# Building the right factors of a fast matrix product on ScalarE and by accumulating DMAs instead of GpSimd, in a two-layer hybrid encoder on one core

## The chip, the core and the metric

The program runs on one core of a Trainium2 chip. A core has five engines that each work through a queue of their own, in order: PE (TensorE, matrix products into PSUM), DVE (VectorE), ACT (ScalarE), POOL (GpSimd) and SP (SyncE, which here only issues DMAs). They meet at semaphores. POOL can issue DMAs as well, and those can add what they carry to what lies at their destination. The metric is the device time of one execution in microseconds (us).

## The reference, cut to what matters

Two layers, 656 tokens (528 of a prompt with 16 meta tokens, 128 of eight running streams), 1024 channels, all in float32. Each layer normalises, projects, runs three kinds of heads and adds an output projection; the change is in what follows, the gated feed-forward part:

```python
h2 = rmsnorm(x, p['g_ffn'])
gate, val = jnp.split(h2 @ p['w_up'].astype(x.dtype), 2, axis=-1)      # 2 x 2816 columns
gate_c, ffn_new = causal_dwconv(gate, ffn_past, p['ffn_conv_w'], p['ffn_conv_b'])   # width 3
x = x + (jax.nn.gelu(gate_c) * val) @ p['w_down'].astype(x.dtype)

def rmsnorm(x, g):
    y = xf * lax.rsqrt(jnp.mean(xf * xf, axis=-1, keepdims=True) + EPS)
    return (y * g.astype(jnp.float32)).astype(x.dtype)
```

## The kernel before

The activations lie with channels on the 128 partitions: eight tiles x0 to x7 of 128 channels by 656 tokens. A float32 product is made of three faster ones: ACT rounds a number to a short format (the high part), DVE subtracts that from the number (the low part), and PE multiplies high by high, high by low and low by high (`mm3`, L374). So every weight tile passes ACT and DVE before PE can use it (`w_split`, L360 and L361; four blocks of 128 columns are one unit). The passing units are held in four buffers (`wsp`, the tiles whi and wlo); a unit that is to stay longer can be put in tiles of the general pool (`own=True`, the tiles ghi and glo). The raw weights come through four buffers (`wraw`), which SP fills.

The feed-forward part of a layer has an entry and a long steady stretch. The steady stretch computes the up-projection in pairs of column blocks (a gate pair, then a value pair) by a seven-product scheme of Winograd's kind: 2 by 2 blocks on either side are first added and subtracted, and seven products take the place of eight. The left factors come from weights (`combos`, L961 on POOL, split at L967 on ACT and L968 on DVE). The right factors come from the activations, once in a layer (`factors`): for each k of 0 to 3 the blocks are b11 and b12 (the first and second half of the tokens of x_k) and b21 and b22 (the same of x_(k+4)). The differences are t1 = b12 - b11, t2 = b22 - t1, t3 = b22 - b12 and t4 = b21 - t2; the seven right factors are b11, b21, t2, t3, t4, t1 and b22, and each is split into high and low parts (ACT at L1065, DVE at L1066, tile fh).

The entry, in the order of the program:

1. The last quarter of the output projection (d_ob), tile by tile. DVE adds it to x (L417), ACT squares x (L408, tile sq), POOL adds up the squares (L413; the last of the adds is DVE's), ACT and DVE split x for the first plain products.
2. PE sums the squares over partitions (np_h), ACT and DVE make the factor r from it (L313 to L317). Meanwhile PE runs the plain products of gates 0 and 1 and value 0 (e_u), whose weights lie in ghi and glo.
3. DVE multiplies x0 to x7 by gain and r (L1044). POOL makes t1 and t2, later t3 and t4 (L1052 to L1061). Two of the seven groups of right factors are split (`FE = 2`); the rest after the plain gates.
4. DVE evicts gates 0 and 1 (L1224), ACT and DVE run the convolution (L1088, L1091) and ACT the gelu (L1094). POOL multiplies by r (L1233), DVE multiplies with the value (L1238 to L1240). Value 1 (d_v), then gates 2 and 3 (d_g) run as plain products on PE. The weights of value 1 take passing buffers, those of gates 2 and 3 ghi and glo.
5. The remaining right factors are split, and PE begins on the seven-product scheme: d_v again, for values 2 and 3, whose products are called v010 to v016 below, then d_g for gates 4 and 5, and between them the down-projection (d_dn).

The order in which the instructions of an engine stand is set by a scheduler from the program's order and its own idea of when inputs are ready; from the seven-product scheme on, the orders of DVE and PE are written out by hand (`manual_schedule`). The DMAs that POOL issues in the before kernel are of the same kind as the new ones: L701 adds one SBUF tile to another, L1306 adds a tile to one in HBM.

Of the kernel before, what the change touches and what calls it, by code (L numbers as in the profile page):

```python
# [12 lines left out]
AF = mybir.ActivationFunctionType  # L13
ALU = mybir.AluOpType
# [7 lines left out]
T = 656  # L22
# [3 lines left out]
NFF = 22  # L26
# [11 lines left out]
NPG = 2  # L38
# [119 lines left out]
def trunk_kernel(ctx: ExitStack, tc: tile.TileContext, i: dict, o: dict, depth: int = 2):  # L158
# [12 lines left out]
    V, A, G, PE = nc.vector, nc.scalar, nc.gpsimd, nc.tensor  # L171

    def S(name, dt=F32):
        return slots.tile([128, T], dt, tag="S", name=name)
# [22 lines left out]
    xs = [S(f"x{m}") for m in range(8)]  # L197
# [25 lines left out]
    def par(name, k):  # L223
        c = COLS[name][0] + k
        return cst[:, c:c + 1]
# [96 lines left out]
    def seq(ins):  # L322

        if start["on"]:
            tc.keep_in_program_order(ins)
            start[ins.ins.engine] = ins.ins

    def split(src, g, nm, a=0):
        hi = S(f"hi_{nm}", F32R)
        lo = S(f"lo_{nm}", F32R)  # L330
        if g is None:
            A.copy(hi[:, a:T], src[:, a:T])  # L332
            V.tensor_tensor(out=lo[:, a:T], in0=src[:, a:T], in1=hi[:, a:T].bitcast(F32), op=ALU.subtract)  # L333
        else:
            seq(A.activation(out=hi[:, a:T], in_=src[:, a:T], func=AF.Identity, scale=g))
            seq(V.scalar_tensor_tensor(out=lo[:, a:T], in0=src[:, a:T], scalar=g, in1=hi[:, a:T].bitcast(F32), op0=ALU.mult,
                                       op1=ALU.subtract))
        return hi, lo

    def w_load(w, k0, kt, parts=None):  # L340
        raw = wraw.tile([128, 8, 128], F32, tag="raw", name="raw")
        for a, b in parts or ((0, kt),):
            nc.sync.dma_start(out=raw[:, a:b], in_=w[:, (k0 + a) * 128:(k0 + b) * 128].rearrange("p (k n) -> p k n", n=128))
        return raw
# [4 lines left out]
    def w_split(raw, kt, a=0, own=False):  # L349

        half = 4 if kt in (4, 8) else 3
        units = []
        while a < kt:
            n = min(half, kt - a)
            if own:
                hi, lo = unit_s("ghi"), unit_s("glo")
            else:
                hi = wsp.tile([128, 4, 128], F32R, tag="whi", name="whi")
                lo = wsp.tile([128, 4, 128], F32R, tag="wlo", name="wlo")
            seq(A.copy(hi[:, :n], raw[:, a:a + n]))  # L360
            seq(V.tensor_tensor(out=lo[:, :n], in0=raw[:, a:a + n], in1=hi[:, :n].bitcast(F32), op=ALU.subtract))  # L361
            units += [(hi, lo, m) for m in range(n)]
            a += n
        return units

    def weights(w, k0, kt, own=False):
        return w_split(w_load(w, k0, kt), kt, 0, own)
# [8 lines left out]
    def gemm1(units, ks, rhs, nm, ab, P=PD):  # L376
        ps = P(f"d_{nm}")
        for k in range(len(ks)):
            mm3(ps, units[k], rhs[ks[k]], ab, k == 0, k == len(ks) - 1)
        return ps  # L380

    def gemm(units, ks, rhs, nm, cc=CA, P=PD):

        return [gemm1(units, ks, rhs, f"{c}_{nm}", cc[c], P) for c in range(2)]

    def gemm_group(unit_lists, ks, rhs, nm, cc=CA):

        ps = [[PD(f"e0_{nm}"), PD(f"e1_{nm}")], [PD(f"e2_{nm}"), PB(f"e3_{nm}")], [PB(f"e4_{nm}"), PB(f"e5_{nm}")]]
        last = len(ks) - 1
        for k in range(len(ks)):  # L390
            for m, units in enumerate(unit_lists):
                for c in range(2):
                    mm3(ps[m][c], units[k], rhs[ks[k]], cc[c], k == 0, k == last)
        return ps
# [7 lines left out]
    sq_acc = {}  # L402

    def sq_add(m, ab=(0, T), E=None):

        a, b = ab
        sq = S(f"sq{m}")
        seq(A.activation(out=sq[:, a:b], in_=xs[m][:, a:b], func=AF.Square))  # L408
        if m == 0:
            sq_acc["t"] = sq  # L410
        else:
            t = sq_acc["t"]
            seq((E or (V if m == 7 else G)).tensor_tensor(out=t[:, a:b], in0=t[:, a:b], in1=sq[:, a:b], op=ALU.add))  # L413

    def add_x(m, ps, cc=CA):
        for c, (a, b) in enumerate(cc):
            V.tensor_tensor(out=xs[m][:, a:b], in0=ps[c][:, :b - a], in1=xs[m][:, a:b], op=ALU.add)  # L417

    def x_out(m):
        nc.sync.dma_start(out=xdr[m], in_=xs[m][:, :T])  # L420
# [616 lines left out]
    def factors(l, r, cc):  # L1037

        (a0, a1), (b0, b1) = cc
        w = a1 - a0  # L1040
        src = []
        for k in range(4):
            for m in (k, k + 4):
                V.scalar_tensor_tensor(out=xs[m][:, a0:T], in0=xs[m][:, a0:T], scalar=par("g_ffn", 8 * l + m),  # L1044
                                       in1=r[:, a0:T], op0=ALU.mult, op1=ALU.mult)
            b11, b12 = xs[k][:, a0:a1], xs[k][:, b0:b1]
            b21, b22 = xs[k + 4][:, a0:a1], xs[k + 4][:, b0:b1]
            t = S(f"ft{l}{k}")
            t1, t3 = t[:, :w], t[:, HC:HC + w]
            t = S(f"fu{l}{k}")  # L1050
            t2, t4 = t[:, :w], t[:, HC:HC + w]
            G.tensor_tensor(out=t1, in0=b12, in1=b11, op=ALU.subtract)  # L1052
            G.tensor_tensor(out=t2, in0=b22, in1=t1, op=ALU.subtract)
            src.append((b11, b21, t2, t3, t4, t1, b22))
        out = [[] for k in range(4)]
        for n in range(7):
            for k in range(4):
                b11, b21, t2, t3, t4, t1, b22 = src[k]
                if n == 1:
                    G.tensor_tensor(out=t3, in0=b22, in1=xs[k][:, b0:b1], op=ALU.subtract)  # L1060
                    G.tensor_tensor(out=t4, in0=b21, in1=t2, op=ALU.subtract)  # L1061
                x = src[k][n]
                t = S(f"fh{l}{k}{n}", F32R)
                hi, lo = t[:, :w], t[:, HC:HC + w]
                A.copy(hi, x)  # L1065
                V.tensor_tensor(out=lo, in0=x, in1=hi.bitcast(F32), op=ALU.subtract)  # L1066
                out[k].append((hi, lo))
            yield out

    def by_stream(x):  # L1070
        return x.rearrange("p (s n) -> p s n", s=8)
# [40 lines left out]
    ks8 = list(range(8))  # L1112
    for l in range(depth):
# [7 lines left out]
        if l == 0:  # L1121
            hs = []
# [20 lines left out]
        ps3 = gemm_group(w3, ks8, hs, f"i{l}")  # L1143
# [21 lines left out]
        for n in range(3, 24):  # L1165
            advance(front)
            ps = gemm(nxt, ks8, hs, f"i{l}{n}")
# [11 lines left out]
        cx, cy = (CB, CC) if l == depth - 1 else (CA, CA)  # L1179
# [7 lines left out]
        for m in range(8):  # L1187
            advance(front)
            x_in(m, xsrc)
            ps = gemm(nxt, ka, mix, f"oa{l}{m}", cx)  # L1190
# [8 lines left out]
        hs = []  # L1199
        wu = i["w_up"][l]  # L1200
        w3 = [weights(wu[n], 0, 8, True) for n in (0, 1, NFF)]
        for m in range(8):
            ps = gemm(nxt, kb, mix, f"ob{l}{m}", cx)
            add_x(m, ps, cx)
            x_out(m)
            sq_add(m, (cx[0][0], T))
            hs.append(split(xs[m], par("g_ffn", 8 * l + m), f"h2{l}{m}", cx[0][0]))
            if m < 7:
                nxt = weights(wo[m + 1], 6, 2)
        r = norm_r(onesd[:, 0], [sq_acc["t"]], f"h2{l}", cx)  # L1210
        ps3 = gemm_group(w3, ks8, hs, f"u{l}", cx)
        gout = S(f"gout{l}")[:, :NFF * 18].rearrange("p (f n) -> p f n", f=NFF)
        wd = i["w_down"][l]
        a0, cw = cy[0][0], cx[0][1] - cx[0][0]
        gates, vals, gts = {}, {}, {}
        fac = factors(l, r, cx)
        for n in range(FE):
            tm = next(fac)
# [7 lines left out]

        for ft in range(2):
            plain_gate(ft, ps3[ft])
        wg = [weights(wu[ft], 0, 8, True) for ft in range(2, 2 + NPG)]
        for ft in range(2):  # L1230
            ps = ps3[2] if ft == 0 else gemm(weights(wu[NFF + 1], 0, 8), ks8, hs, f"v{l}1", cx, PB)
            a, av = gates.pop(ft)
            G.tensor_tensor(out=a[:, a0:TP], in0=a[:, a0:TP], in1=r[:, a0:TP], op=ALU.mult)  # L1233
            G.tensor_tensor(out=av, in0=av, in1=by_stream(r[:, TP:T]), op=ALU.mult)
            v = vals[ft] = S(f"gv{l}{ft}")
            (c0, c1), (d0, _) = cx
            n0 = TP - d0
            V.tensor_tensor(out=v[:, a0:c1], in0=ps[0][:, a0 - c0:c1 - c0], in1=a[:, a0:c1], op=ALU.mult)  # L1238
            V.tensor_tensor(out=v[:, d0:TP], in0=ps[1][:, :n0], in1=a[:, d0:TP], op=ALU.mult)
            V.tensor_tensor(out=by_stream(v[:, TP:T]), in0=by_stream(ps[1][:, n0:n0 + 128]), in1=av, op=ALU.mult)  # L1240
# [87 lines left out]
        for p in range(1, NFF // 2):  # L1328
            for up in (up_gate, up_val)[1 if p == 1 else 0:]:
                for st in up(p):  # L1330
# [3 lines left out]
                    while due and due[0][0] <= nprod:  # L1334
                        _, n, j = due.pop(0)
# [28 lines left out]
        if l < depth - 1:  # L1364
            hs = []
# [10 lines left out]
    for c, (a, b) in enumerate(CF):  # L1376
# [3 lines left out]
        for m in range(8):  # L1380
# [4 lines left out]
            ps = gemm1(wl[m], ks, gts, f"fin{c}{m}", (a, b))  # L1385
# [28 lines left out]
```

## Time and profile before

| | us |
|---|---|
| median of three runs (1696.43 to 1701.21) | 1698.6 |
| the profiled execution | 1697.38 |
| its span, first to last instruction | 1695.6 |
| entry of layer 0, from the last add of step 1 to the first product of step 5 | 393.5 to 439.6 |
| entry of layer 1, the same | 1217.4 to 1262.1 |

The profile is one execution. A row of a timeline gives the start in us from the start of the span, the duration, engine, line, operation, the tiles written and read, the shape, and in brackets how long the engine stood idle before it and what it waited for. Rows of one kind that follow each other are merged, with their count. A duration of a row includes the tail of the last instruction; of instructions that follow each other the next starts some 0.08 us before it ends. PEclk is the granted clock of PE as a share of full speed.

### The profile page before, as it was taken

What the parts mean: (1) busy time and instruction counts of PE and PEld (TensorE: products, weight loads), DVE (VectorE), ACT (ScalarE), POOL (GpSimd) and SP (SyncE); (2) the same over time, 40 slices, a digit from 0 to 9 for tenths busy, and PEclk for the clock granted to TensorE, in tenths of its full rate; (3) what the DMA queues carried; (4) which work ended last, traced back from release to release, by engine and by line L of the source; (5) the groups of instructions that cost most, each with busy time, mean ns of one, the idle gap of its engine ahead of it and who ended that gap; (6) DMA issues with size and microseconds to landing.
All of it is one profiled execution on the core that took longest, in us unless ns stands there. A gap on an engine that the chain in (4) does not pass through costs nothing.

```text
span 1695.6 us, 28745 instructions
## 1 busy us (share of the span) xinstructions
PE 1625.4 (96%) x10772; PEld 1532.0 (90%) x10772; DVE 1238.9 (73%) x2380; ACT 878.7 (52%) x1744; POOL 581.7 (34%) x668
## 2 busy tenths in 40 slices
PE   7999999998999999999999999999999999999985
PEld 6898888898899999999998978789888999999984
DVE  6579985769877767766648898776898767776444
ACT  5656576553545444444445647575454444444343
POOL 0102220008466554553001122100476555554423
PEclk9999999999999999999999999999999999999998
DMA  5236431342145344444612555214411344344442
GB/s 205 90 96 159 115 99 36 112 154 79 50 112 119 100 105 106 102 102 107 221 65 89 128 130 122 67 65 136 144 38 60 95 120 107 101 102 98 119 110 94
DMA packets 75003, 180.56 MB, mean 106 GB/s; under 512 B 12752, under 2 KB 18384, under 8 KB 74864
## 3 DMA queue, kind: packets, MB, share of 16 engines
q1 hardware_dynamic: 62192, 149.36, 27.3%
q0 software_dynamic: 12672, 29.37, 11.1%
q8 instruction: 84, 1.38, 0.3%
q14 instruction: 55, 0.45, 0.1%
HBM read 129.80 MB, written 35.46 MB: 97 GB/s over the span
## 4 chain that ended last, share of the span: by engine, by line
PE 78%; DVE 10%; issue 4%; POOL 3%; ACT 2%; DMA 2%; SPq 0%; DVEq 0%; POOLq 0%; ACTq 0%
PE d_i L374 16%; PE d_dn L374 15%; PE d_v L374 12%; PE d_g L374 12%; PE d_oa L374 5%; PE e_i L374 2%; PE sc L491 2%; DMA x<-x_scr 1%; PE hl L785 1%; PE po L527 1%; PE e_u L374 1%; DVE fh L1066 1%; DVE wlo L361 1%; PE d_ob L374 1%; DVE wlo L968 1%
## 5 line engine op out<-in xcount | busy, mean ns | idle before, releaser
L374 PE MATMUL d_v<-fh,whi 128*128 128x328 f32 (+1 forms) x1120 | 251.6, 312 | 1.4 <-ACT whi L967 1.4
L360 ACT CAST whi<-raw 128x384 fp32r<-128x384 f32 (+2 forms) x243 | 132.5, 548 | 210.1 <-PE d_i L374 75.5
L374 PE MATMUL d_g<-fh,whi 128*128 128x328 f32 (+1 forms) x1008 | 226.5, 312 | 0.3 <-ACT whi L967 0.3
L374 PE MATMUL d_i<-hi_h,whi 128*128 128x328 f32 x672 | 219.0, 326 | 0.0
L374 PE MATMUL d_i<-lo_h,whi 128*128 128x328 f32 x672 | 213.8, 318 | 0.0
L374 PE MATMUL d_i<-hi_h,wlo 128*128 128x328 f32 x672 | 212.8, 317 | 0.0
L374 PE MATMUL d_dn<-hi_g,wlo 128*128 128x328 f32 (+1 forms) x640 | 199.9, 312 | 2.8 <-DVE wlo L361 2.8
L374 PE MATMUL d_dn<-hi_g,whi 128*128 128x328 f32 (+1 forms) x640 | 200.2, 313 | 1.9 <-ACT hi_g L332 1.7
L374 PE MATMUL d_dn<-lo_g,whi 128*128 128x328 f32 (+1 forms) x640 | 200.2, 313 | 1.8 <-DVE lo_g L333 1.8
L361 DVE TENSOR_TENSOR wlo<-raw,whi 128x384 fp32r<-128x384 f32 (+2 forms) x243 | 169.7, 713 | 30.4 <-ACT whi L360 20.5
L374 PEld LDWEIGHTS d_v<-fh,whi 128*128 128x128 f32 x1120 | 189.3, 189 | 1.6 <-ACT whi L967 1.6
L968 DVE TENSOR_TENSOR wlo<-wcb,whi 128x512 fp32r<-128x512 f32 x152 | 129.4, 851 | 75.8 <-ACT whi L967 74.8
L374 PE MATMUL d_v<-fh,wlo 128*128 128x328 f32 (+1 forms) x560 | 175.5, 313 | 3.1 <-DVE wlo L968 3.1
L374 PEld LDWEIGHTS d_g<-fh,whi 128*128 128x128 f32 x1008 | 170.4, 189 | 0.5 <-ACT whi L967 0.5
L374 PE MATMUL d_g<-fh,wlo 128*128 128x328 f32 (+1 forms) x504 | 157.9, 313 | 2.3 <-DVE wlo L968 2.3
L961 POOL TENSOR_TENSOR wcb<-raw 128x512 f32<-128x512 f32 x76 | 111.5, 1468 | 129.2 <-DMA raw<-in_w_up 80.9
L968 DVE TENSOR_TENSOR wlo<-raw,whi 128x512 fp32r<-128x512 f32 x114 | 112.8, 991 | 53.8 <-ACT whi L967 53.5
L967 ACT CAST whi<-wcb 128x512 fp32r<-128x512 f32 x152 | 93.7, 620 | 112.1 <-PE d_g L374 33.3
L374 PEld LDWEIGHTS d_i<-hi_h,whi 128*128 128x128 f32 x672 | 127.1, 189 | 9.6 <-issue 5.2
L374 PEld LDWEIGHTS d_i<-lo_h,whi 128*128 128x128 f32 x672 | 127.3, 189 | 3.8 <-issue 1.3
L374 PEld LDWEIGHTS d_i<-hi_h,wlo 128*128 128x128 f32 x672 | 127.0, 189 | 3.0 <-issue 1.3
L374 PEld LDWEIGHTS d_dn<-hi_g,wlo 128*128 128x128 f32 x640 | 121.1, 189 | 3.5 <-DVE wlo L361 3.5
(385 smaller groups left out, 4053.1 us busy)
## 6 DMA issues: line engine op xcount, KB each, us to landing
raw<-in_w_up SPq DMA_DIRECT2D x88, 512.0 KB, 3.6
raw<-in_w_in SPq DMA_DIRECT2D x45, 512.0 KB, 3.7
raw<-in_w_down SPq DMA_DIRECT2D x48, 384.0 KB, 3.7
x_scr<-x SPq DMA_DIRECT2D x24, 328.0 KB, 3.2
x_scr<-dd POOLq DMA_DIRECT2D x24, 328.0 KB, 4.6
x<-x_scr SPq DMA_DIRECT2D x24, 328.0 KB, 4.3
x_scr<-dd POOLq DMA_DIRECT2D x24, 320.0 KB, 4.5
cvb<-cvt POOLq DMA_DIRECT2D x20, 328.0 KB, 4.9
```

What stands on the lines that cost most here:

```text
L360: seq(A.copy(hi[:, :n], raw[:, a:a + n]))
L361: seq(V.tensor_tensor(out=lo[:, :n], in0=raw[:, a:a + n], in1=hi[:, :n].bitcast(F32), op=ALU.subtract))
L374: PE.matmul(ps[:, :b - a], lhsT=ww[:, n], rhs=r[:, a:b], start=first and j == 0, stop=last and j == 2)
L491: PE.matmul(ps[:, o0:o0 + w], lhsT=q[64 * c:64 * c + 64, q0:q0 + 128], rhs=k[64 * c:64 * c + 64, n * w:(n + 1) * w], start=True, stop=True)
L527: PE.matmul(po[:, :128], lhsT=vt[:, j * 128:(j + 1) * 128], rhs=aT[:, j * 128:(j + 1) * 128], start=j == 0, stop=False)
L785: PE.matmul(ps[:, c * 128:(c + 1) * 128], lhsT=kk[:, 16 + 128 * c:144 + 128 * c], rhs=both(m0 + 64 * c, 64), start=True, stop=True)
L961: G.tensor_tensor(out=t, in0=x, in1=y, op=op)
L967: A.copy(hi, x)
L968: V.tensor_tensor(out=lo, in0=x, in1=hi.bitcast(F32), op=ALU.subtract)
L1066: V.tensor_tensor(out=lo, in0=x, in1=hi.bitcast(F32), op=ALU.subtract)
```

## The change

Three things change, in both layers.

- The sums of squares of step 1 (`sq_dma` takes the place of `sq_add`, in this place alone): POOL no longer adds. Squares 2 and 4 are added to square 0, and 3 and 5 to square 1, by DMAs that POOL issues. DVE adds square 6, the sum in square 1, and square 7 to square 0.
- The differences of the right factors: ACT writes -b11, -b12 and a copy of b11, and DMAs that POOL issues add b12 to the first (t1) and b22 to the second (t3). At the second group a DMA adds t3 to the copy (t2 = b11 + t3), and at the third ACT writes -t2 and a DMA adds b21 (t4). That is 16 ACT instructions and 16 DMAs in a layer for 16 subtractions on POOL.
- The weights of value 1, gate 2 and gate 3 all go through the passing buffers, in the order of their use. Those of value 1 and gate 2 are now asked for ahead of the right factors, and ghi and glo hold the first three units only.

```diff
+    def sq_dma(m, ab):
+        a, b = ab
+        sq = S(f"sq{m}")
+        A.activation(out=sq[:, a:b], in_=xs[m][:, a:b], func=AF.Square)
+        if m < 2:
+            sq_acc[m] = sq
+        elif m < 6:
+            G.dma_start(out=sq_acc[m % 2][:, a:b], in_=sq[:, a:b], accum_op=ALU.add)
+        else:
+            t = sq_acc["t"] = sq_acc[0]
+            if m == 7:
+                V.tensor_tensor(out=t[:, a:b], in0=t[:, a:b], in1=sq_acc[1][:, a:b], op=ALU.add)
+            V.tensor_tensor(out=t[:, a:b], in0=t[:, a:b], in1=sq[:, a:b], op=ALU.add)
...
-            G.tensor_tensor(out=t1, in0=b12, in1=b11, op=ALU.subtract)
-            G.tensor_tensor(out=t2, in0=b22, in1=t1, op=ALU.subtract)
+            A.mul(t1, b11, -1.0)
+            G.dma_start(out=t1, in_=b12, accum_op=ALU.add)
+            A.mul(t3, b12, -1.0)
+            G.dma_start(out=t3, in_=b22, accum_op=ALU.add)
+            A.copy(t2, b11)
...
                 if n == 1:
-                    G.tensor_tensor(out=t3, in0=b22, in1=xs[k][:, b0:b1], op=ALU.subtract)
-                    G.tensor_tensor(out=t4, in0=b21, in1=t2, op=ALU.subtract)
+                    G.dma_start(out=t2, in_=t3, accum_op=ALU.add)
+                if n == 2:
+                    A.mul(t4, t2, -1.0)
+                    G.dma_start(out=t4, in_=b21, accum_op=ALU.add)
...
-            sq_add(m, (cx[0][0], T))
+            sq_dma(m, (cx[0][0], T))
...
+        wv = weights(wu[NFF + 1], 0, 8)
+        wg = [weights(wu[2], 0, 8)]
         fac = factors(l, r, cx)
...
-        wg = [weights(wu[ft], 0, 8, True) for ft in range(2, 2 + NPG)]
+        wg.append(weights(wu[3], 0, 8))
         for ft in range(2):
-            ps = ps3[2] if ft == 0 else gemm(weights(wu[NFF + 1], 0, 8), ks8, hs, f"v{l}1", cx, PB)
+            ps = ps3[2] if ft == 0 else gemm(wv, ks8, hs, f"v{l}1", cx, PB)
```

The order of the instructions follows. In these rows a tile ft holds t1 and t3 of one k, a tile fu holds t2 and t4, and ga00 is the gate-0 tile; in brackets stand the engines and DMA queues that an instruction waits for (DMASW: DMAs issued by POOL, DMAHW: by SP). First ACT, layer 0, between the split of the second group of right factors (fh031) and the gates of step 4. Before:

```order
L1065 CAST fh031_4544<-x7_4006 128x328 [waits DVE_49,Pool_49]
L360 CAST ghi_4575<-raw_4573 128x512
L1088 ACTIVATE ga00_4555<-gp00_4547,cst_82 128x672 [waits DVE_49]
L1088 ACTIVATE ga01_4568<-gp01_4560,cst_82 128x672 [waits DVE_49,Pool_49]
L360 CAST ghi_4579<-raw_4573 128x512 [waits PE_49]
L1094 ACT_TABLE_LOAD
```

Now:

```order
L1086 CAST fh031_4572<-x7_4006 128x328 [waits DVE_49]
L1081 ACTIVATE fu00_4514<-fu00_4514 128x328 [waits DMASW4_49]
L1081 ACTIVATE fu01_4523<-fu01_4523 128x328 [waits DMASW7_49]
L1081 ACTIVATE fu02_4532<-fu02_4532 128x328 [waits DMASW2_49]
L1081 ACTIVATE fu03_4541<-fu03_4541 128x328 [waits DMASW3_49]
L1109 ACTIVATE ga00_4583<-gp00_4575,cst_82 128x672 [waits DVE_49,Pool_49]
L1109 ACTIVATE ga01_4596<-gp01_4588,cst_82 128x672 [waits DVE_49,Pool_49]
L1115 ACT_TABLE_LOAD
```

The negations of the third group (L1081), each of which waits for a DMA, have come to stand ahead of the gates.

POOL, layer 0, from the last left factor (wcb) on; the names are as above. Before, the start of the 16 subtractions:

```order
L961 TENSOR_TENSOR wcb_4873<-raw_4853,raw_4855 128x512
L1052 TENSOR_TENSOR ft00_4493<-x0_3460 128x328 [waits DMASW3_49,DVE_49,PE_49]
L1053 TENSOR_TENSOR fu00_4494<-x4_3850,ft00_4493 128x328 [waits DVE_49,DMASW6_49,PE_49,Pool_49]
L1060 TENSOR_TENSOR ft00_4493<-x4_3850,x0_3460 128x328
L1061 TENSOR_TENSOR fu00_4494<-x4_3850,fu00_4494 128x328 [waits Pool_49]
```

Now, in whole up to the twelfth DMA:

```order
L976 TENSOR_TENSOR wcb_4889<-raw_4869,raw_4871 128x512
L1069 DMA ft00_4513<-x0_3460 128x328 [waits DMASW3_49,PE_49,Activation_49]
L1071 DMA ft00_4513<-x4_3850 128x328 [waits DVE_49,Activation_49]
L1069 DMA ft01_4522<-x1_3598 128x328 [waits PE_49,Activation_49]
L1071 DMA ft01_4522<-x5_3902 128x328 [waits DVE_49,Activation_49]
L1079 DMA fu00_4514<-ft00_4513 128x328 [waits DMAHW0_49,DMASW1_49]
L1069 DMA ft02_4531<-x2_3718 128x328 [waits PE_49,Activation_49]
L1071 DMA ft02_4531<-x6_3954 128x328 [waits DMASW6_49,DVE_49,Activation_49]
L1079 DMA fu01_4523<-ft01_4522 128x328 [waits DMASW7_49,DMASW3_49]
L1069 DMA ft03_4540<-x3_3798 128x328 [waits DMASW0_49,Activation_49]
L1071 DMA ft03_4540<-x7_4006 128x328 [waits DVE_49,Activation_49]
L1079 DMA fu02_4532<-ft02_4531 128x328 [waits DMASW6_49,DMASW2_49,PE_49]
L1079 DMA fu03_4541<-ft03_4540 128x328 [waits DMASW1_49,Activation_49]
```

Each DMA into a tile fu waits until the second DMA into the tile ft of the same number has landed, and holds POOL's queue until then.

DVE, layer 0, the end of step 1, with the adds of squares (sq) among the low parts of x (lo_h) and of weights (wlo, here those of value 1 and gate 2). Before:

```order
L417 TENSOR_TENSOR x7_4006<-d_1_ob07_4310,x7_4006 128x328 [waits PE_49]
L361 TENSOR_TENSOR wlo_4602<-raw_4599,whi_4601 128x512 [waits DMAHW5_49,Activation_49]
L336 SCALAR_TENSOR_TENSOR lo_h206_4294<-x6_3954,cst_82,hi_h206_4293 128x656 [waits DVE_49,Activation_49]
L361 TENSOR_TENSOR wlo_4606<-raw_4599,whi_4605 128x512 [waits Activation_49]
L413 TENSOR_TENSOR sq0_4111<-sq0_4111,sq7_4320 128x656 [waits Activation_49,Pool_49]
```

Now:

```order
L432 TENSOR_TENSOR x7_4006<-d_1_ob07_4309,x7_4006 128x328 [waits PE_49]
L428 TENSOR_TENSOR sq0_4111<-sq0_4111,sq6_4289 128x656 [waits DMASW6_49,Activation_49]
L336 SCALAR_TENSOR_TENSOR lo_h206_4293<-x6_3954,cst_82,hi_h206_4292 128x656 [waits DVE_49,Activation_49]
L427 TENSOR_TENSOR sq0_4111<-sq0_4111,sq1_4140 128x656 [waits DMASW7_49,DVE_49]
L336 SCALAR_TENSOR_TENSOR lo_h207_4324<-x7_4006,cst_82,hi_h207_4323 128x656 [waits Activation_49]
L428 TENSOR_TENSOR sq0_4111<-sq0_4111,sq7_4319 128x656 [waits DVE_49]
L361 TENSOR_TENSOR wlo_4498<-raw_4491,whi_4497 128x512
```

Two adds on DVE now wait for DMAs, with low parts of x queued behind them, and the second low part of value 1's weights follows the last add. Later on DVE the weights of the first two seven-product units, which stood between step 1 and step 2, follow the last right factor (fh036) in the changed kernel.

## Rows read from the trace of the kernel before

**Rows 1.** Page, part 1: span; busy us, share and instructions of each engine.
```profile
span 1695.6 us, 28745 instructions
...
PE 1625.4 (96%) x10772; PEld 1532.0 (90%) x10772; DVE 1238.9 (73%) x2380; ACT 878.7 (52%) x1744; POOL 581.7 (34%) x668
```

**Rows 2.** Windows, layer 0: stretch, length, busy us (instructions) PE PEld DVE ACT POOL, PEclk, DMA share, GB/s.
```profile
380.00:390.00 10.00, 8.41 (x55) 7.98 (x53) 9.81 (x13) 7.07 (x11) 7.69 (x5) 1.00 0.80 284
...
420.00:430.00 10.00, 7.11 (x36) 6.59 (x36) 9.12 (x18) 8.02 (x13) 7.84 (x14) 0.83 0.16 52
```

**Rows 3.** Timeline of PE, layer 0's entry, rows with idle time before them.
```profile
394.45 1.34 PE L312 MATMUL np_h<-sq,onesd 128*128 128x328 f32 x4 [0.90 <-DVE sq L413]
...
423.87 0.64 PE L374 MATMUL d_g<-hi_h,glo 128*128 128x328 f32 x1 [2.41 <-DVE glo L361]
...
448.30 0.57 PE L374 MATMUL d_v<-fh,whi 128*128 128x328 f32 x2 [1.37 <-ACT whi L967]
...
449.35 0.42 PE L374 MATMUL d_v<-fh,wlo 128*128 128x328 f32 x1 [0.48 <-DVE wlo L968]
...
466.67 0.42 PE L374 MATMUL d_dn<-lo_g,whi 128*128 128x328 f32 x1 [1.05 <-DVE lo_g L333]
```

**Rows 4.** Timeline of DVE, layer 0's entry.
```profile
381.93 2.23 DVE L336 SCALAR_TENSOR_TENSOR lo_h<-x,cst,hi_h 128x656 fp32r<-128x656 f32 x1
...
384.90 0.89 DVE L336 SCALAR_TENSOR_TENSOR lo_h<-x,cst,hi_h 128x656 fp32r<-128x656 f32 x1
...
399.07 12.38 DVE L1044 SCALAR_TENSOR_TENSOR x<-x,cst,r_h 128x656 f32<-128x656 f32 x8
...
411.38 8.99 DVE L1066 TENSOR_TENSOR fh<-x,fh 128x328 fp32r<-128x328 f32 x8
...
422.26 0.95 DVE L1091 SCALAR_TENSOR_TENSOR ga<-gp,cst,ga 128x672 f32<-128x672 f32 x1
...
431.77 1.72 DVE L1066 TENSOR_TENSOR fh<-fu,fh 128x328 fp32r<-128x328 f32 x4
...
448.61 0.68 DVE L968 TENSOR_TENSOR wlo<-raw,whi 128x512 fp32r<-128x512 f32 x1
```

**Rows 5.** Timeline of POOL, layer 0's entry.
```profile
385.50 6.09 POOL L413 TENSOR_TENSOR sq<-sq,sq 128x656 f32<-128x656 f32 x3 [2.04 <-ACT sq L408]
...
400.14 1.89 POOL L961 TENSOR_TENSOR wcb<-raw 128x512 f32<-128x512 f32 x1
...
421.07 0.88 POOL L1061 TENSOR_TENSOR fu<-x,fu 128x328 f32<-128x328 f32 x1
...
426.03 2.69 POOL L1233 TENSOR_TENSOR ga<-ga,r_h 128x528 f32<-128x528 f32 x1 [2.16 <-ACT ga L1094]
...
429.52 1.33 POOL L1233 TENSOR_TENSOR ga<-ga,r_h 128x528 f32<-128x528 f32 x1
```

**Rows 6.** Timeline of ACT, layer 0: the first gate.
```profile
421.28 0.95 ACT L1088 ACTIVATE ga<-gp,cst 128x672 f32<-128x672 f32 x1 [8.73 <-DVE gp L1224]
```

**Rows 7.** DMA: L701 by duration in ns, its landings, the smallest transfer, POOL's queue.
```profile
L701 POOL DMA_DIRECT2D cvb<-cvt x20: 845/864/1855, 122.8 to 1046.9; - x20
...
DMA to landing us min/median/max: 3.6/4.9/7.3
...
out_hgrn_p<-hsall SPq DMA_DIRECT2D x8, 16.0 KB, 1.8
...
q0 software_dynamic: 12672, 29.37, 11.1%
```

**Rows 8.** Timelines of POOL, ACT and PE, layer 1's entry.
```profile
1226.33 1.34 POOL L1052 TENSOR_TENSOR ft<-x 128x322 f32<-128x322 f32 x1
...
1244.25 0.94 ACT L1088 ACTIVATE ga<-gp,cst 128x656 f32<-128x656 f32 x1 [7.97 <-DVE gp L1224]
...
1270.97 0.41 PE L374 MATMUL d_v<-fh,wlo 128*128 128x322 f32 x1 [1.27 <-DVE wlo L968]
...
1316.56 0.42 PE L374 MATMUL d_dn<-hi_g,wlo 128*128 128x320 f32 x1 [2.12 <-DVE wlo L361]
```

## The prediction

> **What bounds the kernel now.** I read the page's totals first. PE is busy for 1625.4 of 1695.6 us, so with 10772 matmuls one costs .151 us, and all idle time of PE together is 70 us [rows 1]. A change that takes no matmul away can win only from this idle time and from stretches at a lower clock. So I went on to the stretch that the change touches, by windows: in layer 0 PE is busy for 8.41 of 10 us at 380 to 390 and for 7.11 at 420 to 430, there with a granted clock of 0.83 on average, which is part of the window at 1.2 instead of 2.4 GHz [rows 2]. DVE is full in both. Then the timeline of PE says for what it stands: for the last add of the squares (.90), for the low part glo of gate 2's weights (2.41), for high and low parts of the weights of v014 (1.37 and .48), and at the start of the down-projection for low parts of the gated values (1.05 the last of them) [rows 3]. All are DVE's work or ACT's in front of it, so DVE's timeline is next. A product-and-subtract 656 wide takes .89 us alone and 2.23 beside a POOL add; eight scalings by r take 12.38, that is 1.55 each, and eight low parts of factors 8.99, that is 1.12 each, where four later ones take 1.72, that is .41 each plus a tail [rows 4]. POOL's rows show why: in the same time run six adds of squares (the last three 6.09 us), and from 402.0 to 421.95 its 16 subtractions without a gap [rows 5]. The two engines take turns. The entry is DVE-bound, and DVE is slowed by POOL.
>
> **The change, part by part.**
>
> *Adds of squares.* Removed: six POOL adds, each of which holds up one DVE instruction by up to 1.3 us (2.23 against .89, rows 4). Added: two adds on DVE of about .8, and four DMAs in two chains of two, behind which DVE's last adds wait. The DMA of square 4 goes out when that of square 2 has landed, so two landings pass from square 2 (378.6 by ACT's place in the order) and from square 3 (about 381.1). The nearest row is the kernel's own adding DMA of the same 128x656 tiles: 3.6 us at the least, 4.9 in the middle, 7.3 at most [rows 7]. With 4.9 the later chain lands at 390.9, and with two adds and a low part behind it the sums are done at 393.4; with 3.6 DVE itself decides, near 391.5; with 7.3 it is 398. Before, PE started np_h at 394.45 [rows 3]. Since the DMA engines are already taken to .80 there [rows 2], I expect landings over the middle, 5.3, and take **no change**, bounds -3 and +4 in each layer. A queue of POOL is moved past nothing here: only left factors stand behind.
>
> *Scaling by r and the first eight low parts.* Without the subtractions beside them the eight scalings fall to 8 x .82 plus some 2.2 for the three left factors that POOL still makes there, 8.8 instead of 12.4, and the low parts from 9.0 to 3.4. So DVE is ready for gate 0 at about 411 instead of 420.3: 9 us of DVE are won. They are not won on the path, for now DVE stands idle until ACT has begun the gate.
>
> *The differences.* Removed: 16 subtractions, 20 us of POOL. Added on ACT: 16 pieces of some .4, under which nothing waits but the DMAs. Added on POOL: 16 issues at .864 [rows 7]. The order of ACT decides: the four negations of the third group stand ahead of gate 0, and the last of them waits for the twelfth DMA. That DMA is reached so. POOL's last left factor ends at 402.0 [rows 5]; its raw weights are asked for when a raw buffer falls free, which is now behind the last add of squares and not ahead of it, an add and a low part, 1.3 us, later: 403.3. From there issues come .87 apart, and each DMA into fu waits for the second into its ft. For the landing of half a tile no row stands. From below: 1.8, the smallest transfer [rows 7]. From above: 4.9, the whole tile [rows 7]. POOL's queue used 11.1% of 16 engines over 1695.6 us for 12672 packets, that is .24 us each; a DMA of 128 rows puts some 9 on an engine, 2.1 us, and half-length packets save about 1.05 of the 3.6 to 4.9, which leaves 2.6 to 3.9. The DMA engines are nearly idle in this stretch (.16, rows 2), so I take 3.0. Then fu00 goes out at +3.9, ft03's second half at +8.2, fu03 waits for it until +11.2 and lands at +14.2: 417.5. With 1.8 it is +11.4, with 4.9 it is +19.9. ACT negates (.4) and starts gate 0 at **417.9, where it was 421.28** [rows 6]: 3.4 us earlier. In layer 1 the subtractions began at 1226.33 and the gate at 1244.25 [rows 8]; 1226.3 + 1.3 + 14.2 + .4 = 1242.2, 2.1 us earlier.
>
> The Trainium skill has a price for such a DMA: DMA: Bandwidth & Descriptors, in its anatomy of an SWDGE DMA, fits a fixed 2.0 us plus bytes over 436 GB/s. By that half a tile (164 KB) lands in 2.4 us, an estimate from the page, the twelfth DMA comes 1.4 us earlier in each layer and the whole sum would be 3 us lower; for the whole tile it would say 2.8, and the trace's least is 3.6, so the trace is dearer and is what the sum uses.
>
> *Weights in the passing buffers.* Gate 2's weights are now split ahead of r, so the wait of 2.41 for glo and the slow clock behind it go [rows 3, 2]. What is late next: the weights of the first seven-product units, which were split ahead of r before, now stand on DVE behind the last right factor. From gate 0 to the product with r of gate 1 it took 421.28 to 430.85 [rows 6, 5], 9.6 us; two low parts of glo (.6 each) no longer stand in it and POOL's first product should fall from 2.69 to 1.33 as the second did [rows 5]: 7.0, so 424.9. From there DVE has the value's three pieces (.9 together), two low parts of gate 3's weights (1.2, .6 each with the tail left off, rows 4), 20 low parts of factors (20 x .41 = 8.2), three pieces of gate 2 (.9), two taps of the convolution (1.7 by rows 4), a piece of gate 3 (.4) and then the first unit's low part (.6): 14.0, so 438.9. PE meanwhile has run dry at about 434, which is a new wait of some 5 us, and probably a new short stretch at 1.2 GHz in place of the old one. Four products of 12 matmuls (4 x 1.8 us) bring v014 to 446.1; before it started at 448.30 [rows 3]. **Layer 0: -2.2.** In layer 1 the start is 2.1 instead of 3.4 earlier, so **-.9** against 1270.97 [rows 8].
>
> *What follows v014.* DVE has its right factors behind it in both kernels, but now also the weights of v014 some 3 us before PE needs them, where before PE stood for them (DVE cut them at 448.61, rows 4). So part of the later waits goes. In layer 0 these are .48, .38, .75 and 1.05, the first and the last in rows 3; I take 2.0 of 2.7. In layer 1 there are six behind 1270.97, from .27 to 2.12, the last in rows 8, together 5.7; there DVE is the bound until the down-projection begins, so its lead is what can be won: 3.0 at most, and I take that.
>
> The sum is 2.2 + .9 + 2.0 + 3.0 = 8.1 us. The profiled execution took 1697.38, which is 1.2 under the median of the three runs: 1689.3, and by the median **1690.5 us**.
>
> **Rivals.**
>
> *The landings are later than taken, and nothing is left.* At 4.1 for half tiles the twelfth DMA lands at +17.5 instead of +14.2, and at 5.9 for whole ones the sums come 1.2 later: 4.5 a layer, 9 in all, 1699. For it: two or three of L701's DMAs that follow each other at once land late, up to 7.3, and here up to four are under way. Against: those are whole tiles, and the DMA engines have little else to do at 403 to 418.
>
> *Slower by late landings.* The same place, further on: with 7.3 for whole tiles (the row's worst) in the crowded 380 to 392 the sums are 4 later, and with 5.4 for halves fu03 lands at +21.4, another 7.2. That is 11 a layer, 22 in all, 1712. PE then stands at np_h and again at v010. It decides from about 4.0 for a half tile on, where the gain is gone, and from 4.6 the kernel is slower by more than a measurement's doubt. Against it: the middle of all L701's landings is 4.9 for twice the bytes [rows 7].
>
> *Faster.* Halves land in 2.0 or so; the chain is 2.4 shorter a layer, 1686 or a little less.
>
> *POOL cannot issue while DVE works, so the subtractions' cost stays in another form.* One L701 issue took 1.855 us instead of .864 [rows 7]. If all twelve did, the gate would come 11 us later a layer, 22 in all: 1712. Against it: the other 19 or so of L701 stood near .864 with DVE as full as here, in the convolution's stage. The Trainium skill's SBUF — State Buffer warns of this in its box on DVE blocking DMAs: descriptors that POOL writes starve while DVE runs an operation in a two-port mode; by that rule 1712 would be the time. The median of .864 disagrees for the kinds of DVE instruction that stand here.
>
> **How the numbers follow.** Three runs of this kernel lie within 0.28%, so 0.3%, 5.1 us, is about what can be told from no change. My forecast .58, and its own range is 1685 to 1695; faster still .08; late landings without a gain .18; slower by them .12; starving issues .04. Of the forecast four fifths are over 5.1 us, of the third case three quarters within it. So faster .54, no change .25, slower .21. For 8 in 10 the range is 1683 to 1703: the lower end is the small landing, the upper one the late landings without the worst.
>
> **What would show it.** Right: the POOL row of L1052 to L1061 is gone, the scalings take under 1.2 each, DVE stands idle for some 6 us before the first tap of gate 0 with ACT as what ended it, ACT's L1081 waits for DMAs until about 417.5, and PE stands for the low part of v010's weights for about 5 us while the waits for glo and at v014 are gone. Wrong: np_h starts over 2 us later than 394.45, fu tiles land over 4 us after issue, or the DMA issues on POOL last over 1.2. It would be wrong in kind if PE did not stand before v010, for then DVE was not the bound after the gates.

## The result, and the profile after

The changed kernel took **1711.98 us** (median of six runs, 1710.06 to 1714.50). The kernel before took 1698.31 beside it (1695.18 to 1701.40). The ratio is 1.0086, 95% interval 1.0072 to 1.0100: 13.7 us slower. I had forecast 1690.5. The profiled execution is of 1712.12 us. Ratios, here and below, are formed from fast executions alone and are not those of the medians: one execution of e9 (7874 us) and one of the kernel before that was timed beside e5 to e8 (1963 us) were slow and are left out of them.

The page of the changed kernel, part 1 and the row of POOL's DMA queue:

```profile
span 1710.3 us, 28831 instructions
...
PE 1630.0 (95%) x10772; PEld 1539.5 (90%) x10772; DVE 1220.5 (71%) x2384; ACT 891.1 (52%) x1776; POOL 557.3 (33%) x664
...
q0 software_dynamic: 18432, 37.36, 13.9%
```

PE is 4.6 us busier with the same matmuls, at a mean granted clock of .980 for .985 before, and stands 10.1 us longer [rows 1]. The two sum to the 14.7 by which the span grew. PE's timeline shows where it stands, first in layer 0, then in layer 1:

```profile
397.21 2.52 PE L312 MATMUL np_h<-sq,onesd 128*128 128x328 f32 x4 [7.31 <-DVE sq L428]
...
447.29 0.64 PE L374 MATMUL d_v<-fh,wlo 128*128 128x328 f32 x1 [3.80 <-DVE wlo L983]
...
1229.23 1.41 PE L312 MATMUL np_h<-sq,onesd 128*128 128x322 f32 x2 [8.15 <-DVE sq L428]
...
1278.42 0.42 PE L374 MATMUL d_v<-fh,wlo 128*128 128x322 f32 x1 [4.00 <-DVE wlo L983]
...
1330.41 0.64 PE L374 MATMUL d_dn<-hi_g,wlo 128*128 128x320 f32 x1 [2.12 <-DVE wlo L361]
```

The last of these rows is the same wait as the last of [rows 8], 13.85 us later. So nearly all of the loss has come about by then, in the two entries. Starts of different traces have to be compared by their place in the stage, for layer 0's began earlier here. These are the first products of the last quarter of the output projection, before and now:

```profile
370.80 0.32 PE L374 MATMUL d_ob<-hi_mx,whi 128*128 128x328 f32 x1
...
369.21 0.32 PE L374 MATMUL d_ob<-hi_mx,whi 128*128 128x328 f32 x1
```

From there np_h is 28.0 us away instead of 23.6 [rows 3], 4.4 more; in layer 1 it is 28.6 instead of 24.2, again 4.4 more. The first product of the down-projection comes 8.4 later in its place in layer 0 and 7.4 in layer 1. So a little over half of the loss has come about by np_h, and the rest behind it. The wait at np_h was .90 in layer 0 [rows 3] and is 7.31; it is 8.15 in layer 1. What it stands for is on DVE, and before that on POOL, whose rows at L423 are the DMAs of squares 2 to 5:

```profile
385.19 0.49 DVE L432 TENSOR_TENSOR x<-d_ob,x 128x328 f32<-128x328 f32 x1
393.05 0.84 DVE L428 TENSOR_TENSOR sq<-sq,sq 128x656 f32<-128x656 f32 x1 [7.37 <-DMA sq<-sq]
...
396.23 0.84 DVE L428 TENSOR_TENSOR sq<-sq,sq 128x656 f32<-128x656 f32 x1
```

```profile
378.03 0.89 POOL L423 DMA_DIRECT2D sq<-sq  x1 [24.97 <-PE d_ob L374]
380.22 0.86 POOL L423 DMA_DIRECT2D sq<-sq  x1 [1.30 <-ACT sq L419]
386.01 0.88 POOL L423 DMA_DIRECT2D sq<-sq  x1 [4.93 <-ACT sq L419]
389.41 0.88 POOL L423 DMA_DIRECT2D sq<-sq  x1 [2.52 <-DMA sq<-sq]
...
401.98 1.40 POOL L976 TENSOR_TENSOR wcb<-raw 128x512 f32<-128x512 f32 x1 [11.69 <-DMA raw<-in_w_up]
```

Square 3's DMA goes out at 380.22, and the DMA of square 5 behind it can go at 389.41 only: 9.2 us. DVE meets its first such add at 393.05 with nothing done since 385.7. All eight landings of this kind, from the view of line L423:

```profile
DMA to landing us min/median/max: 5.2/7.4/8.6
```

And the stretch by windows (columns as in [rows 2]):

```profile
380.00:390.00 10.00, 9.91 (x65) 9.46 (x63) 5.45 (x10) 7.61 (x12) 2.33 (x3) 1.00 1.04 316
390.00:400.00 10.00, 2.79 (x6) 1.98 (x7) 6.07 (x9) 1.23 (x3) 0.29 (x1) 0.74 0.50 109
```

At 380 to 390 PE works nearly all the time (8.41 before). DVE is done with its work at 385.7, with low parts at .90 each, and stands for the rest of the window, hence 5.45 instead of 9.81. That part of the change does what it should. But the DMA engines are full, 1.04 where it was .80 [rows 2], and then PE has 2.79 us of work in ten, at a mean granted clock of .74 in that window.

### The profile page after: what moved, and what is told of

Same layout as the page of the kernel before. It is cut to its first block, busy times and chain, and to the rows that moved or that the text cites. A ratio compares the mean times of both kernels' runs of the same rounds, so it can differ in the third digit from the quotient of the medians.

```text
span 1710.3 us, 28831 instructions
## 1 busy us (share of the span) xinstructions
PE 1630.0 (95%) x10772; PEld 1539.5 (90%) x10772; DVE 1220.5 (71%) x2384; ACT 891.1 (52%) x1776; POOL 557.3 (33%) x664
## 3 DMA queue, kind: packets, MB, share of 16 engines
q0 software_dynamic: 18432, 37.36, 13.9%
## 5 line engine op out<-in xcount | busy, mean ns | idle before, releaser
L360 ACT CAST whi<-raw 128x384 fp32r<-128x384 f32 (+2 forms) x251 | 137.5, 550 | 210.8 <-PE d_i L374 76.0
L983 DVE TENSOR_TENSOR wlo<-raw,whi 128x512 fp32r<-128x512 f32 x114 | 116.7, 1025 | 51.1 <-ACT whi L982 50.8
```

## The experiments

Ratios are to the kernel before, timed on the same chip in the same session.

| kernel | us | ratio, 95% interval |
|---|---|---|
| e1, sums alone | 1712.3 | 1.0087 (1.0070 to 1.0104) |
| e2, differences alone | 1699.3 | 1.0010 (.9999 to 1.0020) |
| e3, weights alone | 1696.9 | .9997 (.9988 to 1.0006) |
| e4, changed, without the sums | 1700.8 | 1.0017 (1.0005 to 1.0029) |
| e5, sums on VectorE | 1696.3 | .9996 (.9985 to 1.0007) |
| e6, two squares by DMA | 1703.4 | 1.0029 (1.0018 to 1.0041) |
| e7, sums alone, early writes | 1706.9 | 1.0050 (1.0035 to 1.0065) |
| e8, e4 with the gates first | 1699.0 | 1.0005 (.9994 to 1.0017) |
| e9, e8 without the weights | 1694.4 | .9981 (.9969 to .9993) |
| e10, e9 with VectorE sums | 1694.0 | .9987 (.9976 to .9997) |
| e11, e10 with the weights | 1700.9 | 1.0022 (1.0012 to 1.0032) |
| e12, e9 with early gate copies | 1685.6 | .9935 (.9922 to .9947) |

### Which part it is: e1 to e4

Theory A was the late sums, B the weights' place, C the chain of half-tile DMAs before the gates. e1 to e3 put one hunk of the change each into the kernel before; e1 is the one line

```diff
-            sq_add(m, (cx[0][0], T))
+            sq_dma(m, (cx[0][0], T))
```

and e4 takes that line out of the changed kernel.

**e1.** 

> The kernel before with only the sums of squares by accumulating DMAs. Theory A (the DMAs of the squares land after 7 to 9 us instead of 5.3, so PE stands some 7 us at np_h in each layer): np_h starts 2.8 us later than 394.45 in layer 0 and some 4.4 later, by its place in the layer, in layer 1; this delay stays to the end, so 1698.3 + 7 = 1705. Theory B (the weights in the passing buffers do the harm): the late r falls into waits that are there anyway, 1698 to 1700. Theory C (the chain of half-tile DMAs in front of the gates does it): 1698 to 1700 too.

**e2.** 

> The kernel before with only the right factors' differences by ScalarE and DMAs. Theory A: the twelfth DMA lands some 17.8 us after the first issue, 402.0 + 17.8 = 419.8, and gate 0 starts near 420.3 where it was 421.28: about 1 us a layer won, 1696 to 1698. Theory B: the same. Theory C: PE's waits for gate 2's and the first units' weights grow, 1703 or more.

**e3.** 

> The kernel before with only the weights of value 1 and gates 2 and 3 in the passing buffers. Theory A: the wait of 2.41 for glo goes, and PE waits as long for the low parts of the first unit: no change, 1697 to 1701. Theory B: PE stands for the first unit's low part by 4 to 6 us a layer, 1707 or more. Theory C: as A.

**e4.** 

> The changed kernel with the sums of squares as before (adds by GpSimd). Theory A: np_h is back at its place, and half or more of the 13.7 us is gone: 1703 to 1706. Theory B and C: little of it is gone, 1709 to 1712.

The sums alone make as much as the whole loss, and more than theory A asked (1712 for 1705). B and C fall as its cause: the weights alone change nothing, the differences alone cost at most .2%. But e2 also misses what A gave it: 1699.3 for 1696 to 1698, so the differences won nothing. By the ratios e4 gives 11.7 of the 14.6 us back, more than A asked (1700.8 for 1703 to 1706). The 2.9 that are left are what the differences and the weights cost together.

### Why the sums land late, and what their wait holds: e5 to e7

e6 is e1 with `elif m < 4` for `elif m < 6`. The others:

```diff
# e5, from before
-            sq_add(m, (cx[0][0], T))
+            sq_add(m, (cx[0][0], T), V)
# e7, from e1: x_out(m) stands behind the first part of the out-projection
             ps = gemm(nxt, ka, mix, f"oa{l}{m}", cx)
             add_x(m, ps, cx)
+            x_out(m)
...
-            x_out(m)
             sq_dma(m, (cx[0][0], T))
```

**e5.** 

> The kernel before with all seven adds of squares on VectorE: no add on GpSimd and no DMA. Theory A (the loss is the wait for DMAs; VectorE without GpSimd beside it has room for six adds of .8): PE's waits of 1.04 and 1.59 in the last eight products of the out-projection go as they did in the changed kernel, and np_h starts 2 to 3 us earlier than in the kernel before: 1690 to 1694. Rival (the adds are too much for VectorE, which is why they have to lie elsewhere): 1697 or more, with PE waiting for x.

**e6.** 

> The kernel with the sums alone, but only squares 2 and 3 added by DMA; 4 to 7 on VectorE. Theory A (two late landings pass one after the other in each chain): with one landing in a chain, and two DMAs less on the engines, both land by 387 and np_h starts near 392: 1692 to 1698. Rival (any VectorE add behind a DMA costs this much): 1706 or more.

**e7.** 

> The kernel with the sums alone, with the eight writes of x made in the first part of the out-projection, before its last two products are added (this leaves those products out of the residual that is written). Theory A (the accumulating DMAs land late since the 16 DMA engines are full at 378 to 392 with these writes and with weights): they land after 5 to 6 us instead of 7 to 9 and np_h starts 3 to 4 us earlier than with the sums alone: 1702 to 1706. Rival (they are slow by themselves): they land as late as before, 1710 or more.

e7 moves 2.6 MB of writes a layer out of the stretch. Its DMA share at 380 to 390 and its landings:

```profile
380.00:390.00 10.00, 9.57 (x62) 9.03 (x60) 5.48 (x10) 7.75 (x12) 2.16 (x3) 1.00 0.86 187
380.00:385.00 5.00, 5.00 (x35) 5.00 (x34) 4.37 (x8) 4.15 (x7) 0.41 (x1) 1.00 0.99 245
385.00:390.00 5.00, 4.57 (x29) 4.03 (x27) 1.11 (x3) 3.60 (x6) 1.76 (x2) 1.00 0.72 129
```

```profile
DMA to landing us min/median/max: 3.7/5.4/7.9
```

```profile
393.73 1.47 PE L312 MATMUL np_h<-sq,onesd 128*128 128x328 f32 x4 [4.15 <-DVE sq L428]
```

The middle landing falls from 7.1 in e1 to 5.4, which is near the 5.3 that I had taken, and np_h starts 3.4 us earlier than in e1 (397.09), though the stage began .2 later. By single landings of layer 0, squares 2 and 3 still take 6.9 and 7.2 us, issued where the share is .99; squares 4 and 5 take 3.7 and 3.9 where it is .72, against 6.8 and 5.9 in e1 at 1.04 (385 to 390). SP's own writes of x, too, land after 6.3 to 7.8 us in the changed kernel's stage and after 2.2 to 4.1 in the same stage before. So the landings are late since the engines are full, and 5 to 6 us of e1's loss hang on that.

The other 8 or 9 remain, although np_h is then only .7 later in its place than before (24.4 us behind the stage's first product, 23.6 before). I have not taken them apart by a run, but the traces show a path. The second low part of value 1's weights stands on DVE close to the last add of squares, behind it in e7 (394.31) and ahead of it before (392.87), and SP's load of the left factors' raw weights waits for this low part. So the left factors start at 398.56 instead of 397.04, 3.0 later by their place in the stage. POOL's 16 subtractions follow, and behind them the small copies for the gates. Gate 1, before and in e7:

```profile
422.42 0.95 ACT L1088 ACTIVATE ga<-gp,cst 128x672 f32<-128x672 f32 x1 [0.19 <-POOL gp L1078]
...
424.89 0.95 ACT L1103 ACTIVATE ga<-gp,cst 128x672 f32<-128x672 f32 x1 [3.74 <-POOL gp L1093]
```

Ahead of this gate PE waits 3.17 for glo in layer 0 (2.41 before), behind it .79 for the next ghi, and 2.62 for a high part in the seven-product scheme (1.37 before [rows 3]). From np_h to the first product of the down-projection, before and in e7:

```profile
394.45:462.63 68.18, 63.06 (x396) 61.18 (x397) 63.64 (x91) 30.45 (x59) 44.38 (x49) 0.97 0.11 36
...
393.73:465.76 72.03, 64.84 (x391) 62.91 (x391) 65.92 (x93) 31.71 (x61) 45.06 (x50) 0.93 0.11 34
```

That is 3.9 us more, 2.1 of them waits of PE and the rest longer products, at a mean granted clock of .93 for .97.

e6 has only one DMA in each chain, yet it lands later than I thought (7.1/8.2/9.0), and its verdict rests on where DVE meets it:

```profile
386.48 0.84 DVE L428 TENSOR_TENSOR sq<-sq,sq 128x656 f32<-128x656 f32 x1 [4.66 <-DMA sq<-sq]
```

```profile
388.69 0.61 PE L374 MATMUL d_ob<-hi_mx,whi 128*128 128x328 f32 x1 [5.64 <-DVE x L432]
```

The add stands in DVE's queue ahead of adds of x. PE waits 5.64 us for x, not for the sum. Neither expectation fits: it is better than e1 and worse than no DMA. e5 takes no DMA and lands between its two expectations. np_h starts at 392.48 without a wait, but the stage also began earlier, at 368.68, so that its place is as before (23.8 us on, 23.6 before): PE waits 2.10 for x instead, with six adds more on DVE. The adds are worth about the same on either engine.

### Where the differences' gain went: e8 to e12

e2 shows it. ACT begins gate 0 and gate 1 at

```profile
422.21 0.94 ACT L1109 ACTIVATE ga<-gp,cst 128x672 f32<-128x672 f32 x1
...
425.64 0.95 ACT L1109 ACTIVATE ga<-gp,cst 128x672 f32<-128x672 f32 x1 [2.48 <-POOL gp L1099]
```

Behind np_h (396.61 in e2) that is 25.6 us for gate 0, against 26.8 before [rows 3, 6], a gain. But gate 1 waits for a small copy on POOL that stands behind the third group's four DMAs. The table load for the gelu stands behind gate 1 on ACT. e8 to e11 hold the third group behind the gates; e12 also moves the copies:

```diff
# e8 from e4, e9 from e2; e10 and e11 with e5's sums; mark: gate 1's gelu and its last copy
             plain_gate(ft, ps3[ft])
+        with tc.issue_after(mark["gelu"].ins), tc.issue_after(mark["copy"].ins):
+            tm = next(fac)
# e12, from e9
+        early = [gate_in(l, ft, gpast, a0) for ft in range(2)]
         fac = factors(l, r, cx)
...
-            g, gs_ = gate_in(l, ft, gpast, a0)
+            g, gs_ = early[ft] if ft < 2 else gate_in(l, ft, gpast, a0)
```

In e9, e10 and e12 the split of gate 2's and 3's weights (into ghi and glo, as before) stands ahead of these lines.

**e8.** 

> The changed kernel with the sums as before, and with the third group of right factors (ScalarE's negations and GpSimd's DMAs) held behind the first two gates. Theory (the gain of the differences was eaten since gate 1's copies on GpSimd and gate 0 on ScalarE stand behind the third group's DMAs): gate 0 starts at about 417 instead of 422 and its pair follows, so 3 us a layer come back against 1700.8: 1693 to 1697. Rival (what is late is VectorE's work on the first units' weights, whatever the gates do): 1699 to 1701.

**e9.** 

> Only the differences changed, sums and weights as before, the third group of right factors behind the first two gates and behind the split of gate 2's weights. Theory (with the differences alone the gates won nothing since ScalarE's negations and GpSimd's DMAs stood ahead of them, 1699): gate 0 starts 4 to 5 us earlier in its place in the layer, the wait of 2.41 for glo goes, and 2 to 3 us a layer are won: 1692 to 1695. Rival (PE's later waits, for the first units' weights, take it all): 1697 to 1699.

**e10.** 

> As the run with the gates first and without the weights, and with all sums on VectorE: no DMA waits in the sums, no gate behind a factor's DMA. If both effects add: about 1 us less than without the VectorE sums, 1691 to 1694, faster than the kernel before and the changed one. Rival as there: 1696 to 1699.

**e11.** 

> The changed kernel in all but two things: the sums on VectorE, and the third group behind the gates. Theory: 1712 less the 12 that the sums' DMAs cost and less 2 for the gates: 1696 to 1698; PE still stands for the first unit's weights, which the passing buffers make late. Rival (the weights' place costs nothing): as the run without the weights, 1691 to 1694.

**e12.** 

> As the run with the gates first and without the weights, with the past columns of gates 0 and 1 written by GpSimd ahead of the chain of DMAs. Theory (in that run gate 1 still waited 3.75 us for GpSimd's copy, which stood behind the twelfth DMA): gate 1 follows gate 0 at once, near 415.5 instead of 419.2, and the waits for the first units' low parts at 441.10 and 446.34 shrink: 1690 to 1693, faster than both kernels by over 0.2%. Rival (those low parts stand behind VectorE's factors, whose DMAs set them): 1694 to 1695, no more than there.

e8 comes out as its rival has it, although gate 0 starts at 411.88, before the 417 of its theory; gate 1 waits 4.31 for POOL's copy. e9 gains as its theory said. e10 is no better; e5 alone had gained nothing clear of noise (.9996), so there was nothing to add. e11 against e10 shows that the weights' place does cost once the gates are early: 7 us, more than expected. Then PE stands for the first unit's high part, which ACT cuts late, and once more for the low part:

```profile
438.18 0.57 PE L374 MATMUL d_v<-fh,whi 128*128 128x328 f32 x2 [3.61 <-ACT whi L967]
...
442.14 0.64 PE L374 MATMUL d_v<-fh,wlo 128*128 128x328 f32 x1 [3.40 <-DVE wlo L968]
```

In e9 gate 0 was early, and gate 1 still stood behind POOL's chain. In e12 both follow each other, the first row of e9, the second of e12:

```profile
419.23 0.95 ACT L1111 ACTIVATE ga<-gp,cst 128x672 f32<-128x672 f32 x1 [3.75 <-POOL gp L1099]
```

```profile
412.08 1.83 ACT L1111 ACTIVATE ga<-gp,cst 128x672 f32<-128x672 f32 x2 [1.23 <-DVE gp L1248]
```

```profile
420.00:430.00 10.00, 10.00 (x69) 10.00 (x68) 9.70 (x22) 6.45 (x17) 7.39 (x11) 1.00 0.63 129
```

The last row is e12's window that had 7.11 and a granted clock of .83 before [rows 2]: PE works through, at full clock. In e9 it does so too; what goes in e12 are e9's waits for low parts at values 2 and 3, the longest of layer 0 and of layer 1 being

```profile
446.34 0.42 PE L374 MATMUL d_v<-fh,wlo 128*128 128x328 f32 x1 [1.36 <-DVE wlo L983]
...
1263.39 0.42 PE L374 MATMUL d_v<-fh,wlo 128*128 128x322 f32 x1 [2.37 <-DVE wlo L983]
```

e12 takes 1685.6 us, .9935 of the kernel before. It beats both. I had expected 1690 to 1693; waits that went in e12 did not bring one after them, and the granted clock is 1.00 over both entries (370 to 480, 1190 to 1320).

## Why the prediction was wrong, step by step

**Sums of squares, "I expect landings over the middle, 5.3, and take no change": wrong, and the step that turned a gain into a loss.** By the ratios the kernel is 14.6 us slower where I had 8.1 faster. Of these 22.7, e4 puts 11.7 on the sums; the other 11.0 are the gain of the differences and of the weights, which did not come, and the little that they cost. The landing was 7.4 in the middle. Three things were missed. One is the sum of the traffic: I read the DMA share of .80 as some room, but SP's writes and weights took it, and four adding DMAs with some 2 us of all engines each came on top. The Trainium skill says in DMA: Bandwidth & Descriptors, under issuing engines not being separate queues, that DMAs of all issuers run on the same 16 engines and interleave. The trace agrees: the share is 1.04, and e7 takes 1.7 us off a landing by moving SP's writes. The second is that PE now reaches np_h earlier: it had used up its products by 389.9 and stood there (7.31). I had bounded the loss at +4 in a layer. By np_h's start it was 4.4 in its place in each layer, a little over that.

The third is what comes behind np_h. In e1's trace, which is 12.9 us longer than that of before, np_h is 4.3 and 3.8 later in its place, 8.1 together; the rest came behind. "A queue of POOL is moved past nothing here: only left factors stand behind" was where this was lost: the left factors start at 401.98 instead of 397.04 ([rows 5] has their end), and so all of POOL's chain behind them, and PE works at the lower clock behind its wait (.92 for .97 in e1, from np_h to the down-projection of layer 0). I had let a late np_h cost what it is late, with no term for either.

**Scalings and first low parts: near.** I had 8.8 and 3.4:

```profile
402.26 9.57 DVE L1059 SCALAR_TENSOR_TENSOR x<-x,cst,r_h 128x656 f32<-128x656 f32 x8
...
412.66 3.37 DVE L1087 TENSOR_TENSOR fh<-x,fh 128x328 fp32r<-128x328 f32 x8 [0.82 <-ACT fh L1086]
...
426.19 3.85 DVE L1112 SCALAR_TENSOR_TENSOR ga<-gp,cst,ga 128x672 f32<-128x672 f32 x4 [8.40 <-ACT ga L1109]
```

The last row is the idle time before the first tap, with ACT as what ended it, 8.4 us where I had said some 6.

**Differences, "P0 = 403.3, landing 3.0, gate 0 at 417.9": the middle landing right, the chain wrong.** The views of the lines of t1 and of t2's DMA (L1069, L1079); that of t3 (L1071) has 2.9/3.3/4.3:

```profile
DMA to landing us min/median/max: 2.9/3.0/4.6
```

```profile
DMA to landing us min/median/max: 2.8/3.1/3.9
```

The Trainium skill's fit (DMA: Bandwidth & Descriptors, its anatomy of an SWDGE DMA) gives an estimate of 2.4 for half a tile, and the least here is 2.8. P0 was 407.02, 3.7 later than taken, and 2.8 of that is np_h's. fu03 went out 14.9 later instead of 11.2, and gate 0, the last of these rows, began at 425.22:

```profile
407.02 0.88 POOL L1069 DMA_DIRECT2D ft<-x  x1
...
414.74 0.87 POOL L1079 DMA_DIRECT2D fu<-ft  x1 [0.27 <-issue]
415.90 0.86 POOL L1069 DMA_DIRECT2D ft<-x  x1 [0.29 <-DVE fh L1087]
...
421.95 0.86 POOL L1079 DMA_DIRECT2D fu<-ft  x1 [2.85 <-DMA ft<-x]
...
425.22 0.94 ACT L1109 ACTIVATE ga<-gp,cst 128x672 f32<-128x672 f32 x1
```

An issue lasts .87 as I took it, and the next starts 1.15 later, with .3 of idle time before it that I had not counted. The last DMA into ft03 (417.06) landed after 4.3 us, the slowest of its kind, and fu03, which waits for it, went out 4.9 us behind it. In this stretch too the DMA engines were busy, by the chain itself (the window of 410 to 415):

```profile
410.00:415.00 5.00, 5.00 (x35) 5.00 (x35) 4.18 (x9) 4.58 (x13) 3.73 (x5) 1.00 0.97 149
```

I had called them nearly idle from a row of before; twelve half tiles at 1.05 us of all engines each, half of what I had worked out for a whole one, fill 12.6 of the 15 us. POOL's queue bears this out: its share rose from 11.1% [rows 7] to 13.9% for 8 whole and 32 half tiles more, some 1.0 us a half. Then a step was missing: POOL's copies for gate 1 stand behind the third group's DMAs (e2), and with that group out of the way still behind the twelfth DMA (e9). Even without the late sums the differences gained nothing (e2).

**Weights: the places right, the gain wrong.** The wait for glo went, and PE stood before v010 for 3.80 (I said 5). But a wait as long as that for glo came back one gate later, for the low part of gate 3's weights, 2.47 in layer 0 and 2.40 in layer 1; the sum had no term for it:

```profile
434.46 0.42 PE L374 MATMUL d_g<-hi_h,wlo 128*128 128x328 f32 x1 [2.47 <-DVE wlo L361]
```

The waits at v014 and in the down-projection of layer 0 went too. In layer 1 the later waits, 5.7 before, fell by 1.5 to 4.2, where I had taken 3.0. But alone the part is worth nothing (e3), and with early gates it costs 7 us (e11).

**Rivals.** "Slower by late landings", 1712 at .12, is nearest to what came: its place in the sums, and half of its mechanism. That its time came out is luck: 7.2 of its 11 us a layer are for half tiles that land after 5.4, and they took 2.8 to 4.6; in their place stand the gains that did not come. Starving issues did not come where they were to: 854 to 892 ns at L423, with DVE at work, and at most 1.18 us in the twelve ahead of the gates. Only in the third group, among POOL's small copies, did issues last up to 1.73 us. No run shows why; before, two of L701's twenty lasted 1.73 and 1.86, one right behind the other. The marks that I had set worked: np_h over 2 us late was the first of the three that were to show me wrong.

## What to carry to other kernels

A DMA that takes over an engine's add has two prices: its share of the 16 engines in that very stretch, and the place of the instruction that waits for it in an in-order queue. Before moving work there, add the new transfers' engine time to the DMA share of the window, and follow what else stands behind the waiting instruction. When a part frees 9 us of an engine and the time does not move, look for the smallest thing queued behind it: a memset and a copy on POOL, .1 and .2 us in e12, held back some 8 us of gain here by the ratios of e9 and e12.

## What the runs showed of the hardware

An adding DMA of a 128x656 float32 tile landed after 3.6 us at the least [rows 7] and 9.0 at most, later where the DMA engines were fuller (3.7 and 3.9 at a share of .72 in e7, 5.9 and 6.8 at 1.04 in e1); a half tile after 2.8 to 4.6 in the changed kernel. Leaving out the DMAs of squares 4 and 5 (e6) did not make those of squares 2 and 3 land sooner: 7.5 and 8.9 in layer 0, 7.4 and 8.5 in e1. But in e1 the two later ones go out only when an earlier one has landed, so no run here tells what the number in flight does.
